# The first half's norm ahead of the shift's tiles, and the post-norm, gemv and attention steps around it re-placed

## The chip, the cores and the metric

The kernel runs on one core of a Trainium2 chip. The metric is device microseconds of one execution. A profiled execution gives the trace, whose times are microseconds from the start of its span.

## What is computed

One inference step of a trunk of two layers with D = 1024, over 640 tokens: 512 latent and 128 context. Every layer is a half-step SwiGLU FFN, a token mixer (layer 0 a Fourier mix, layer 1 attention), and another half-step FFN. Every one of these six sublayers (n = 0 to 5) sits between two RMS norms, with shift, scale and gate from a modulation vector:

```python
def _rmsnorm(x, g):
    return x * lax.rsqrt(jnp.mean(x * x, axis=-1, keepdims=True) + RMS_EPS) * g

def _modulated_prenorm(x, g, m, k):
    return _rmsnorm(x, g) * (1 + m[:, 3 * k + 1, None]) + m[:, 3 * k, None]

def _swiglu(h, w1, w2):
    gate, up = jnp.split(h @ w1, 2, axis=-1)
    return (jax.nn.silu(gate) * up) @ w2

def _half_ffn(x, m, k, g_pre, g_post, w1, w2):
    h = _modulated_prenorm(x, g_pre, m, k)
    return x + 0.5 * m[:, 3 * k + 2, None] * _rmsnorm(_swiglu(h, w1, w2), g_post)
```

Here `m = silu(cond) @ w_mod + b_mod` holds nine vectors of 1024 per layer and condition.

## The kernel before, in words

**Layout.** Activations lie transposed, channels on partitions in 8 chunks of 128, tokens along the row. The tokens are worked in two halves of 320; half 1 goes one stage behind half 0, so that one half's norms run beside the other half's matmuls. Every fp32 product is three matmuls (`mm3`, L215 to L217): a weight block and an activation block are each split into `hi` (a rounded copy, made by ACT: L195 for weights, L209 for activations) and `lo` (the rest, a subtraction on DVE: L196, L210), and hi*hi, hi*lo and lo*hi are added. A weight comes in units of 128x1024 (512 KB) by DMA on SP's queue; `unit` sends them up to three ahead of use.

**The beginning** (`begin`, L286). First the scale and the shift of sublayer 0 are needed: 16 tiles of `w_mod_k`, 512 KB each, eight of the scale (idx 1), then eight of the shift (idx 0). TensorE multiplies each as it lands (L299, 4 matmuls of 256 columns). After the scale's tiles half 0's x is loaded on SP's queue (L316, four transfers); its squares (ACT L377, L380), their sum (TensorE L419) and the spread of the inverse root (TensorE L428, after DVE L422 and POOL L423) are put between the shift's tiles, after k = 4 and 6. After tile 16 come ACT L305, TensorE L308, DVE L312 and the coefficients (L358); then per pair of chunks x times the root (DVE L453), times scale plus shift (DVE L459, ACT L461), and the split (ACT L209, DVE L210).

**The first FFN products.** `w1((0, 1), half)` takes four units at once through `multi`, which goes chunk by chunk over all four.

**The norms** (`inverse_rms`, L404) are generators: `yield` gives a time in ns of TensorE work after which the next step is put into the stream, so the sum, the spread and the scaling get places between matmuls. `pre` is the norm ahead of a sublayer, `post` the one behind it. With `in_turn` the sum and the spread keep their place behind the last matmul issued.

**The FFN's tail.** Two late blocks (f = 20, 21, `LATE`) keep a third operand, mixed weights, which `send` splits as a unit of kind "mix" when `tail` asks for it. `behind` lets background work (256 gemv instructions of the modulation, DVE L345, two to a job, one job being one `w_mod_t` tile) run along the w2 passes: 36, 28, 32 and 8 jobs for n = 0, 2, 3 and 5.

**Attention.** `products` makes q and k of the first two pairs for half 0; their evictions (DVE L910, L929, ACT likewise) are issued right behind the matmuls. Then two quads of v follow, while half 1's post norm of sublayer 3 and pre norm of sublayer 4 are finished.

Of the kernel before, what the change touches and what calls it, by code (L numbers as in the profile page):

```python
# [18 lines left out]
P = 128  # L19
# [90 lines left out]
class Kernel:  # L110
# [54 lines left out]
    def send(self, kind, src):  # L165

        nc, two, one = self.nc, slice(512, UNIT), slice(0, 512)
        at = slice(0, UNIT)  # L170
        if kind in ("plain", "block", "gate"):
            raw = self.raw_tile(src)
            self.fast["gate"] = raw
        elif kind == "sums":
            up, gate = self.raw_tile(src), self.fast["gate"]
            raw = self.raw.tile([P, UNIT], F32, tag="raw", name=self.name("sums"))
            nc.vector.tensor_tensor(raw[:, one], gate[:, one], up[:, one], op=ALU.add)
            nc.vector.tensor_tensor(up[:, one], up[:, one], up[:, two], op=ALU.add)
            nc.vector.tensor_tensor(raw[:, two], gate[:, one], up[:, one], op=ALU.add)
            self.fast["up"], self.fast["sums"] = up, raw  # L180
        elif kind in ("up", "u2"):
            raw = self.fast["up"]
            at = at if kind == "up" else two
        elif kind == "mix":
            raw = self.mixed.pop(0)
# [5 lines left out]
        if kind in ("block", "mix"):  # L191
            hi, lo = (self.ring(F32R)[:, :n] for _ in range(2))
        else:
            hi, lo = (self.wts.tile([P, UNIT], F32R, tag=tag, name=self.name(tag))[:, :n] for tag in ("hi", "lo"))
        nc.scalar.activation(hi, raw[:, at], AF.Copy)  # L195
        nc.vector.tensor_tensor(lo, raw[:, at], hi.bitcast(F32), op=ALU.subtract)  # L196
        if kind == "u2":
            nc.vector.scalar_tensor_tensor(out=raw[:, two], in0=self.fast["sums"][:, two], scalar=-1.0,
                                           in1=self.fast["gate"][:, two], op0=ALU.mult, op1=ALU.subtract)
            self.mixed.append(raw)  # L200
        return hi, lo

# [83 lines left out]
    def begin(self):  # L286


        nc, io = self.nc, self.io
        self.new_x(0)  # L290
        ps = self.bank("turn")
        sel = self.ident.rearrange("p (j r) -> p j r", j=4)[:, :, :2]
        for idx in (1, 0):
            out = ps[:, idx * 256 : (idx + 1) * 256]
            for k in range(NCH):
                raw = self.wts.tile([P, UNIT], F32, tag=("hi", "lo")[k % 2], name=self.name("first"))
                nc.sync.dma_start(out=raw, in_=io["w_mod_k"][idx, k])
# [24 lines left out]
        for c in range(0, NCH, 2):  # L322
            nc.sync.dma_start(out=self.xpair(0, c, 1), in_=io["x"][:, c : c + 2, HALF:])
        nc.sync.dma_start(out=self.wide, in_=io["cond_rows"].unsqueeze(0).to_broadcast([P, 2, D]))
        self.later = [partial(nc.scalar.activation, self.wide, self.wide, AF.Silu)]
        self.launch(1, self.pre(0, 0, 1), 4000)

# [75 lines left out]

    def inverse_rms(self, acc):  # L404

# [3 lines left out]
        if not final:  # L409
            with high():  # L410
                nc.vector.tensor_tensor(acc[:, 0], acc[:, 0], acc[:, 1], op=ALU.add)
            acc = [acc[:, 0]]
            yield 1800
        in_turn = lambda: self.tc.issue_after(self.latest.ins) if self.latest else ExitStack()
# [9 lines left out]
        yield 2200  # L424
        ps = self.bank("sum")
# [11 lines left out]

    def pre(self, layer, sub, half, acc=None):

# [25 lines left out]
    def post(self, layer, sub, half, acc, last):  # L465

        nc = self.nc
        lo, hi = SPAN[half]
        r = yield from self.inverse_rms(acc)
        final = type(r) is tuple  # L470
# [19 lines left out]
    def ffn(self, layer, which, base, boundary):  # L490
# [4 lines left out]
        begun = [False, False]  # L495
        g, sums, kept = {}, {}, {}
        quad = lambda t: t.rearrange("p (c t) -> p c t", c=4)
# [5 lines left out]
        def w1(fs, half):  # L503
# [3 lines left out]
            pss = []  # L507
            if len(fs) == 1:
                for j in range(2):
                    pss.append(self.proj(self.unit(base + self.w1_at[fs[0]] + j), lambda k: k * P, half,  # L510
                                         kind="score" if fs[0] == 2 else "main"))
            else:
                pss = self.multi([self.unit(base + self.w1_at[f] + j) for f in fs for j in range(2)], half)
# [39 lines left out]
        def product(f, ps, unit, at, x, start):  # L553
            w = self.unit(base + self.w1_at[f] + unit)
# [50 lines left out]
        def tail(f):  # L605
            a, q = kept[f]
            mix = self.mix_at[f] - self.w1_at[f]
            two(f, a, q, one(f, a, mix), mix, 512)

# [27 lines left out]
        for op, a, half in self.ffn_plan:  # L637
# [29 lines left out]
    def plan_ffn(self):  # L667
# [8 lines left out]
        for f in FAST:  # L676
            plan += [("fast", f, None)]
            if f == SLICES[due][1]:
                for m in range(NCH):
                    plan += [("w2", (due, m), 0), ("w2", (due, m), 1)]  # L680
                due += 1
        plan += [("x", None, None)]
        for half in (0, 1):
# [4 lines left out]
        self.ffn_plan = plan  # L688
        self.ffn_units, self.w1_at, self.w2_at, self.mix_at = [], {}, {}, {}
        for op, v, half in plan:  # L690
            if op == "fast":
                self.w1_at[v] = len(self.ffn_units)
                self.ffn_units += [("gate", v, 0), ("sums", v, 1)]
                self.ffn_units += [(kind, None, None) for kind in (("u2",) if v in LATE else ("up", "all"))]
            elif op == "tail":
                self.mix_at[v] = len(self.ffn_units)
                self.ffn_units += [("mix", None, None)]
            elif op == "w1":
# [181 lines left out]
    def attention(self, base, boundary):  # L880
# [91 lines left out]
        def products(jobs, half=None):  # L972

            todo = []
            for job in jobs:
# [5 lines left out]
            for k in range(NCH):  # L981
                for ps, w, t in todo:
# [8 lines left out]
            with self.tc.high_priority():  # L991
                for job, (ps, w, t) in zip(jobs, todo):
                    if t is None:
                        {"q": query, "k": key}[job[0]](job[1], half, ps)
                    else:
                        v_out(job[1], t, ps)

# [4 lines left out]
        for c in (0, 1):  # L1002
            open_pair(c)
            cached(c)
        products([("q", 0), ("k", 0), ("q", 1), ("k", 1)], 0)
# [5 lines left out]
        products([("q", 0), ("k", 0), ("v", 0, 3), ("v", 0, 4)], 1)  # L1011
        double(0)
# [265 lines left out]
```

## Time and profile before

| | |
|---|---|
| median of the runs | 2323.05 us |
| lowest, highest (3 runs) | 2320.82, 2323.87 us |
| the profiled execution | 2319.2 us |
| its span | 2317.4 us |
| mean granted clock of TensorE | 0.995 |
| TensorE busy | 98% |
| VectorE (DVE), ScalarE (ACT) busy | 75%, 55% |

The profiled execution is 1.8 us longer than its span, and 3.85 us under the median. In the rows below a line of a timeline is: start, time, engine, line, operation, output and inputs, partitions and shape, number of instructions, and in brackets how long the engine was idle before it and what ended that.

### The profile page before, as it was taken

To read this page: it belongs to the slowest core of one execution; us is meant where nothing else is said; L and a number is where in the kernel's file an instruction comes from. 1 tells how busy PE (TensorE), PEld (TensorE's weight loads), DVE (VectorE), ACT (ScalarE), POOL (GpSimd) and SP (SyncE) were. 2 spreads that over 40 slices of the span, in tenths; PEclk is the share of its full clock that TensorE was granted. 3 is DMA by queue.
4 is the path that set the end of the run, shared out by engine and by line. 5 is a ranking of instruction groups with operands and counts; after the bars stand their busy time and mean duration, and the time that the engine had idled before them with its cause. 6 is when DMAs were issued, how large, how long until landed. Compare 5 with 4: busy or idle time off the path is not lost.

```text
span 2317.4 us, 39267 instructions
## 1 busy us (share of the span) xinstructions
PE 2260.0 (98%) x15660; PEld 2209.5 (95%) x15660; DVE 1731.6 (75%) x3006; ACT 1275.8 (55%) x2456; POOL 46.5 (2%) x64
## 2 busy tenths in 40 slices
PE   6999999999999999999999999989999999999997
PEld 4999999999999999999999999988988899999997
DVE  4888888688787787768978887777667485766664
ACT  4445544565654554556545554657667664545544
POOL 0000000000000000000000000010000000000000
PEclk9999999999999999999999999999999999999998
DMA  8234443524333433353243442524333223322332
GB/s 299 94 110 154 147 129 108 182 86 122 125 107 103 139 123 119 112 174 127 86 131 121 146 120 99 189 75 147 101 101 100 83 74 101 110 92 82 101 108 75
DMA packets 80280, 278.12 MB, mean 120 GB/s; under 512 B 8800, under 2 KB 15200, under 8 KB 79968
## 3 DMA queue, kind: packets, MB, share of 16 engines
q1 hardware_dynamic: 79824, 275.29, 36.6%
q8 instruction: 122, 2.00, 0.3%
q14 instruction: 62, 0.51, 0.1%
q10 hardware_dynamic: 272, 0.33, 0.0%
HBM read 264.04 MB, written 11.53 MB: 119 GB/s over the span
## 4 chain that ended last, share of the span: by engine, by line
PE 87%; DVE 4%; ACT 4%; DMA 3%; issue 1%; POOL 0%; SPq 0%; DVEq 0%; ACTq 0%; POOLq 0%
PE main L215 25%; PE main L217 25%; PE main L216 25%; PE score L215 3%; PE score L217 3%; PE score L216 3%; DMA raw<-in_w 2%; DVE lo L196 1%; PE sum L428 1%; PE turn L1093 1%; ACT hi L195 1%; PE sum L1109 1%; DMA first<-in_w_mod_k 1%; PE sum L419 1%; PE score L1067 1%
## 5 line engine op out<-in xcount | busy, mean ns | idle before, releaser
L215 PE MATMUL main<-ring,hi 128*128 128x320 f32 x3872 | 1203.7, 312 | 9.6 <-ACT ring L209 9.6
L216 PE MATMUL main<-ring,hi 128*128 128x320 f32 x3872 | 1197.4, 310 | 0.2 <-DVE ring L210 0.2
L217 PE MATMUL main<-ring,lo 128*128 128x320 f32 x3872 | 1195.3, 309 | 1.6 <-DVE lo L196 1.6
L215 PEld LDWEIGHTS main<-ring,hi 128*128 128x128 f32 x3872 | 726.7, 188 | 16.5 <-ACT ring L209 11.8
L216 PEld LDWEIGHTS main<-ring,hi 128*128 128x128 f32 x3872 | 727.8, 188 | 1.6 <-DVE ring L210 0.9
L217 PEld LDWEIGHTS main<-ring,lo 128*128 128x128 f32 x3872 | 726.8, 188 | 1.9 <-DVE lo L196 1.9
L195 ACT ACTIVATE hi<-raw 128x1024 fp32r<-128x1024 f32 (+1 forms) x366 | 355.4, 974 | 445.0 <-PE main L216 372.0
L196 DVE TENSOR_TENSOR lo<-raw,hi 128x1024 fp32r<-128x1024 f32 (+1 forms) x366 | 408.2, 1118 | 139.6 <-ACT hi L195 138.5
L345 DVE SCALAR_TENSOR_TENSOR junk<-raw,wide 128x1024 bf16<-128x1024 f32 x256 | 312.6, 1221 | 16.3 <-DMA raw<-in_w_mod_t 13.7
L631 ACT ACTIVATE y<-main 128x320 f32<-128x320 f32 x320 | 137.3, 431 | 152.1 <-PE main L217 151.2
L196 DVE TENSOR_TENSOR lo<-sums,hi 128x1024 fp32r<-128x1024 f32 x72 | 88.0, 1222 | 60.7 <-ACT hi L195 60.7
L619 ACT ACTIVATE main<-y 128x320 f32<-128x320 f32 x256 | 111.5, 439 | 33.2 <-DVE left L600 26.2
L215 PE MATMUL score<-ring,hi 128*128 128x320 f32 x416 | 128.6, 309 | 0.0
L216 PE MATMUL score<-ring,hi 128*128 128x320 f32 x416 | 128.5, 309 | 0.0
L217 PE MATMUL score<-ring,lo 128*128 128x320 f32 x416 | 128.5, 309 | 0.0
L195 ACT ACTIVATE hi<-sums 128x1024 fp32r<-128x1024 f32 x72 | 76.3, 1060 | 28.7 <-PE main L216 17.4
L215 PE MATMUL main<-ring,ring 128*128 128x320 f32 x288 | 90.1, 313 | 0.0
L216 PE MATMUL main<-ring,ring 128*128 128x320 f32 x288 | 89.2, 310 | 0.0
L217 PE MATMUL main<-ring,ring 128*128 128x320 f32 x288 | 89.2, 310 | 0.0
L381 DVE TENSOR_TENSOR total<-total,square 128x640 f32<-128x640 f32 x71 | 58.2, 822 | 40.4 <-ACT square L380 38.7
L574 DVE TENSOR_TENSOR left<-left,main 128x320 f32<-128x320 f32 x72 | 35.0, 486 | 59.5 <-PE main L217 59.5
L216 PEld LDWEIGHTS score<-ring,hi 128*128 128x128 f32 x416 | 78.1, 188 | 0.0
(177 smaller groups left out, 2654.2 us busy)
## 6 DMA issues: line engine op xcount, KB each, us to landing
raw<-in_w SPq DMA_DIRECT2D x264, 512.0 KB, 3.6
raw<-in_w_mod_t SPq DMA_DIRECT2D x128, 512.0 KB, 4.0
raw<-in_qkv SPq DMA_DIRECT2D x26, 512.0 KB, 3.6
first<-in_w_mod_k SPq DMA_DIRECT2D x16, 512.0 KB, 8.7
spill<-ring SPq DMA_DIRECT2D x12, 640.0 KB, 3.5
ring<-spill SPq DMA_DIRECT2D x12, 640.0 KB, 7.3
raw<-in_bias SPq DMA_DIRECT2D x16, 448.0 KB, 3.4
raw<-in_four_in SPq DMA_DIRECT2D x8, 512.0 KB, 3.5
```

The costliest lines, as they stand in the source:

```text
L195: nc.scalar.activation(hi, raw[:, at], AF.Copy)
L196: nc.vector.tensor_tensor(lo, raw[:, at], hi.bitcast(F32), op=ALU.subtract)
L215: mm(out, whi, xhi, start=start, stop=False)
L216: mm(out, whi, xlo, start=False, stop=False)
L217: self.latest = mm(out, wlo, xhi, start=False, stop=stop)
L345: last = self.nc.vector.scalar_tensor_tensor(out=self.junk, in0=raw, scalar=1.0, in1=self.wide[:, cond, :], op0=ALU.mult, op1=ALU.mult, ac ...
L381: nc.vector.tensor_tensor(acc, acc, sq, op=ALU.add)
L419: nc.tensor.matmul(ps[:, j : j + 1], acc[0][:, t : t + P], self.mean, start=True, stop=True)
L428: self.spread = nc.tensor.matmul(ps[:, t : t + P], col[:, j : j + 1].to_broadcast([P, P]), self.ident, start=True, stop=True)
L574: tt(a, q, z, op=ALU.subtract)
L619: nc.scalar.activation(ps[:, :HALF], self.y[:, m, lo:hi], AF.Copy)
L631: nc.scalar.activation(self.y[:, m, lo:hi], ps[:, :HALF], AF.Copy)
```

## The change

It loads half 0's x first, on ACT's queue, and works its norm in a generator `first`, whose steps are put between the scale's tiles (after k = 3, 5 and 7). After the scale's coefficients y is multiplied by the scale; after the shift's, the shift is added in the split itself: ACT writes `hi` = t + shift, DVE writes `lo` = (t + shift) - hi. The y that the FFN needs later gets its shift from eight ACT instructions in `later`. The first unit of weights is asked for after the shift's tile k = 4, so its transfer goes ahead of the last three tiles. Half 1's norm waits 6500 ns where it waited 1800. For half 0 of sublayer 0 the four w1 units go one by one. The late blocks' mixed weights are split right behind the last slice but one. The background jobs are spread over 64 w2 passes where it was 72. `post` of half 1 waits 2800 ns ahead of the spread where it was 2200 (not behind the mixers). In attention the evictions of the first q and k are called ahead of the second quad.

```diff
 def begin(self):
         self.new_x(0)
+        for c in range(0, NCH, 2):
+            nc.scalar.dma_start(out=self.xpair(0, c, 0), in_=io["x"][:, c : c + 2, :HALF])
+        chain = self.first()
+        next(chain)
...
-                if idx == 0 and k in (4, 6):
-                    self.step(0)
+                if idx == 1 and k in (3, 5, 7):
+                    next(chain)
+                if idx == 0 and k == 4:
+                    self.unit(0, 0)
...
-            if idx:
-                for c in range(0, NCH, 2):
-                    nc.sync.dma_start(out=self.xpair(0, c, 0), in_=io["x"][:, c : c + 2, :HALF])
-                self.launch(0, self.pre(0, 0, 0), 0)
-                self.step(0)
-        with self.tc.high_priority():
-            self.finish(0)
-        self.unit(0, 3)
...
+            with self.tc.high_priority():
+                next(chain, None)
+        with self.tc.issue_after(load.ins), self.tc.issue_after(self.shifted.ins):
+            self.unit(0, 3)
...
+        self.launch(1, self.pre(0, 0, 1, fold=6500), 4000)
+
+    def first(self):
...
+        r = yield from self.inverse_rms(acc)
+        for c in range(0, NCH, 2):
+            nc.vector.tensor_tensor(self.pair(self.y, c, 0), self.xpair(0, c, 0),
+                                    r[:, :HALF].unsqueeze(1).to_broadcast([P, 2, HALF]), op=ALU.mult)
+        yield
...
+                nc.vector.tensor_scalar(t, t, scale, None, op0=ALU.mult)
+            else:
+                nc.scalar.activation(t, t, AF.Copy, scale=scale)
+        yield
+        for c in range(NCH):
+            t, shift, scale = part(c)
+            hi, lo = h.chunk(c, 0)
+            self.shifted = nc.scalar.activation(hi, t, AF.Identity, bias=shift)
+            nc.vector.scalar_tensor_tensor(out=lo, in0=t, scalar=shift, in1=hi.bitcast(F32), op0=ALU.add,
+                                           op1=ALU.subtract)
+        self.later = [partial(nc.scalar.activation, t, t, AF.Identity, bias=shift)
+                      for t, shift, scale in map(part, range(NCH))]
...
 def post(self, layer, sub, half, acc, last):
-        r = yield from self.inverse_rms(acc)
+        r = yield from self.inverse_rms(acc, 2800 if half and sub != 1 else 2200)
...
 def w1(fs, half):
-            if len(fs) == 1:
+            if len(fs) == 1 or n == half == 0:
+                for f in fs:
+                    for j in range(2):
+                        w = self.unit(base + self.w1_at[f] + j)
+                        with self.tc.issue_after(self.latest.ins):
+                            pss.append(self.proj(w, lambda k: k * P, half, kind="score" if f == 2 else "main"))
...
+            elif op == "mix":
+                mixes[a] = self.mix()
...
-                if a[0] < len(SLICES) - 1 or half == 0:
+                if a[0] < len(SLICES) - 1:
                     passed += 1
-                    due = min(BEHIND[n], BEHIND[n] * passed // (2 * NCH * (len(SLICES) - 1) + (NCH if n < 5 else 0)))
+                    due = BEHIND[n] * passed // (2 * NCH * (len(SLICES) - 1))
...
+        put = products([("q", 0), ("k", 0), ("q", 1), ("k", 1)], 0)
         for quad in (1, 0):
             while not self.normed[1][1 - quad]:
                 self.step(1)
+            if quad == 0:
+                put()
             v_tiles(quad, (0, 1), early, "score")
```

How the instructions lie on three engines, before and after. First ACT at the beginning, from the copy of the inverse root (L432, now L467) to the second weight split (L195, now L194); L305 (now L316) copies a product with `w_mod_k`. Before:

```order
L432 ACTIVATE rms_31_235<-sum_30_231 128x320
L305 ACTIVATE left_33_243<-turn_6_106 128x256
L195 ACTIVATE hi_40_278<-raw_39_276 128x1024
L461 ACTIVATE y_78<-y_78,coef_83 128x320 x2
L209 ACTIVATE ring_35_255<-y_78 128x640 x2
L461 ACTIVATE y_78<-y_78,coef_83 128x320 x2
L209 ACTIVATE ring_37_267<-y_78 128x640 x2
L195 ACTIVATE hi_43_284<-raw_42_282 128x1024
```

After:

```order
L467 ACTIVATE rms_20_170<-sum_19_166 128x320
L316 ACTIVATE left_23_188<-turn_10_122 128x256
L352 ACTIVATE y_78<-y_78,coef_83 128x320 x4
L194 ACTIVATE hi_31_239<-raw_30_237 128x1024
L316 ACTIVATE left_36_261<-turn_10_122 128x256
L357 ACTIVATE ring_38_270<-y_78,coef_83 128x320 x4
L357 ACTIVATE ring_40_280<-y_78,coef_83 128x320 x4
L194 ACTIVATE hi_43_292<-raw_42_290 128x1024
```

The root, the scale's multiplications and the first weight split now stand ahead of the shift's L316; behind it only the eight L357 remain.

Second DVE in attention, from the last eviction of the first q and k (L929, now L965) to the fold of half 1's squares for sublayer 4's norm (L411, now L446). L381 (now L416) adds squares, L477 and L479 (now L512 and L514) are the post norm's x times root and its addition. Before:

```order
L929 TENSOR_TENSOR ring_2226_15839<-main_2239_15865,ring_2226_15839 64x192
L381 TENSOR_TENSOR total_2247_15939<-total_2247_15939,square_2248_15961 128x640
L477 TENSOR_TENSOR y_78<-y_78,rms_2246_15926 128x2x320
L196 TENSOR_TENSOR lo_2242_15869<-raw_2240_15866,hi_2241_15868 128x1024
L479 TENSOR_TENSOR ring_2145_15241<-ring_2145_15241,y_78 128x2x320
L196 TENSOR_TENSOR lo_2255_16031<-raw_2253_16028,hi_2254_16030 128x1024
L381 TENSOR_TENSOR total_2247_15939<-total_2247_15939,square_2249_15981 128x640
L381 TENSOR_TENSOR total_2247_15939<-total_2247_15939,square_2250_16022 128x640
L954 COPY square_2251_16026<-score_2259_16040 128x128
L411 TENSOR_TENSOR total_2247_15939<-total_2247_15939 128x320
```

After:

```order
L965 TENSOR_TENSOR ring_2226_15855<-main_2239_15881,ring_2226_15855 64x192
L416 TENSOR_TENSOR total_2247_15958<-total_2247_15958,square_2248_15980 128x640
L416 TENSOR_TENSOR total_2247_15958<-total_2247_15958,square_2249_16003 128x640
L195 TENSOR_TENSOR lo_2242_15885<-raw_2240_15882,hi_2241_15884 128x1024
L416 TENSOR_TENSOR total_2247_15958<-total_2247_15958,square_2250_16014 128x640
L195 TENSOR_TENSOR lo_2255_16023<-raw_2253_16020,hi_2254_16022 128x1024
L446 TENSOR_TENSOR total_2247_15958<-total_2247_15958 128x320
```

The evictions still stand ahead of the squares' additions. The last pair's L477 and L479, which stood between the two, now stand ahead of the evictions, and a copy (L954) is behind the fold.

Third TensorE behind those squares: their sum (L419, now L454) and spread (L428, now L463); the rest are v's matmuls. Before:

```order
L217 MATMUL score_2260_16067<-hi_2237_15861,ring_2220_15827 128x256
L419 MATMUL sum_2261_16094<-mean_86,total_2247_15939 128x1 x3
L215 MATMUL score_2273_16128<-hi_2241_15868,ring_2210_15762 128x256
L216 MATMUL score_2273_16128<-lo_2242_15869,ring_2210_15762 128x256
L428 MATMUL sum_2263_16101<-ident_85,col_2262_16098 128x128 x3
```

After:

```order
L222 MATMUL score_2260_16059<-hi_2237_15877,ring_2220_15843 128x256
L454 MATMUL sum_2261_16086<-mean_86,total_2247_15958 128x1 x3
L463 MATMUL sum_2263_16093<-ident_85,col_2262_16090 128x128 x3
L220 MATMUL score_2273_16144<-hi_2241_15884,ring_2210_15778 128x256
L221 MATMUL score_2273_16144<-lo_2242_15885,ring_2210_15778 128x256
```

The two matmuls between the sum and the spread are gone.

## Rows read from the trace of the kernel before

**Rows 1.** Part 1 of the page: busy time, share of the span, instructions of an engine.

```profile
PE 2260.0 (98%) x15660; PEld 2209.5 (95%) x15660; DVE 1731.6 (75%) x3006; ACT 1275.8 (55%) x2456; POOL 46.5 (2%) x64
```

**Rows 2.** Timeline of TensorE (PE) at the beginning.

```profile
25.07 1.08 PE L299 MATMUL turn<-first,right 128*32 128x256 f32 x8 [0.21 <-DMA first<-in_w_mod_k]
...
29.32 1.65 PE L428 MATMUL sum<-ident,col 128*128 128x128 f32 x6
30.89 1.08 PE L299 MATMUL turn<-first,right 128*32 128x256 f32 x8
...
36.43 0.64 PE L215 MATMUL main<-ring,hi 128*128 128x320 f32 x1 [2.92 <-ACT ring L209]
...
39.54 0.64 PE L217 MATMUL main<-ring,lo 128*128 128x320 f32 x1 [1.60 <-DVE lo L196]
39.97 0.47 PE L215 MATMUL main<-ring,hi 128*128 128x320 f32 x1
40.24 0.47 PE L216 MATMUL main<-ring,hi 128*128 128x320 f32 x1
...
42.64 0.39 PE L217 MATMUL main<-ring,lo 128*128 128x320 f32 x1
...
51.88 0.93 PE L428 MATMUL sum<-ident,col 128*128 128x128 f32 x6 [1.59 <-POOL col L423]
```

**Rows 3.** Timeline of TensorE: spreads of two post norms, then one pre norm's end.

```profile
489.50 0.93 PE L428 MATMUL sum<-ident,col 128*128 128x128 f32 x6 [0.63 <-POOL col L423]
...
1078.42 0.94 PE L428 MATMUL sum<-ident,col 128*128 128x128 f32 x6 [0.71 <-POOL col L423]
...
1099.12 0.80 PE L419 MATMUL sum<-mean,total 128*128 128x1 f32 x6
...
1105.60 0.85 PE L215 MATMUL main<-ring,hi 128*128 128x320 f32 x4 [0.85 <-ACT ring L209]
```

**Rows 4.** Timeline of TensorE in attention.

```profile
1538.08 0.28 PE L217 MATMUL score<-hi,ring 128*128 128x256 f32 x1
...
1544.72 1.41 PE L419 MATMUL sum<-mean,total 128*128 128x1 f32 x6 [6.37 <-DVE total L411]
...
1547.45 1.65 PE L428 MATMUL sum<-ident,col 128*128 128x128 f32 x6 [0.68 <-POOL col L423]
...
1549.97 0.41 PE L216 MATMUL score<-lo,ring 128*128 128x256 f32 x1
```

**Rows 5.** SP's queue at the beginning: its DMA issues.

```profile
1.65 4.32 SPq L297 DMA_DIRECT2D first<-in_w_mod_k  x8
```

**Rows 6.** Windows: stretch, length, busy PE, PEld, DVE, ACT, POOL, clock, DMA share, GB/s.

```profile
20.00:25.00 5.00, 4.27 (x32) 0.75 (x32) 1.45 (x3) 0.00 (x0) 0.00 (x0) 1.00 1.02 409
170.00:180.00 10.00, 10.00 (x70) 10.00 (x70) 6.51 (x10) 5.25 (x8) 0.00 (x0) 1.00 0.57 166
```

**Rows 7.** Timeline of DVE: first modulation copy behind tile 16; fold of sublayer 2's pre norm.

```profile
33.54 0.17 DVE L312 COPY mod<-score 128x8 f32<-128x8 f32 x1 [0.51 <-PE score L308]
...
34.36 0.16 DVE L358 TENSOR_TENSOR coef<-mod,vec 128x8 f32<-128x8 f32 x1
...
1098.49 0.48 DVE L411 TENSOR_TENSOR total<-total 128x320 f32<-128x320 f32 x1
```

**Rows 8.** Groups of ACT by form: busy us, mean ns; one pointer operand (L401).

```profile
L401 ACT ACTIVATE y<-y,coef 128x320 f32<-128x320 f32 x48 | 24.9, 555 | 0.6
```

**Rows 9.** Timeline of DVE in attention.

```profile
1522.10 1.23 DVE L196 TENSOR_TENSOR lo<-raw,hi 128x1024 fp32r<-128x1024 f32 x1 [0.22 <-ACT hi L195]
1524.31 0.82 DVE L477 TENSOR_TENSOR y<-y,rms 128x640 f32<-128x640 f32 x1 [0.98 <-ACT rms L432]
...
1532.92 0.99 DVE L910 SCALAR_TENSOR_TENSOR ring<-main,ring 64x320 fp32r<-64x320 f32 x2
...
1537.62 0.83 DVE L381 TENSOR_TENSOR total<-total,square 128x640 f32<-128x640 f32 x1
```

**Rows 10.** Part 5 of the page, background jobs: busy us, mean ns, idle before.

```profile
L345 DVE SCALAR_TENSOR_TENSOR junk<-raw,wide 128x1024 bf16<-128x1024 f32 x256 | 312.6, 1221 | 16.3 <-DMA raw<-in_w_mod_t 13.7
```

More of the change, by code (lines that the diff above doesn't have):

```diff
@@ L190, in send @@
         n = at.stop - at.start
-        if kind in ("block", "mix"):
+        if kind == "block":
             hi, lo = (self.ring(F32R)[:, :n] for _ in range(2))
@@ L200, in send, with mix @@
             self.mixed.append(raw)
+        return hi, lo
+    def mix(self):
+        raw = self.mixed.pop(0)
+        hi, lo = (self.ring(F32R)[:, :UNIT] for _ in range(2))
+        self.split(hi, lo, raw)
         return hi, lo
@@ L296, in begin @@
                 raw = self.wts.tile([P, UNIT], F32, tag=("hi", "lo")[k % 2], name=self.name("first"))
-                nc.sync.dma_start(out=raw, in_=io["w_mod_k"][idx, k])
+                load = nc.sync.dma_start(out=raw, in_=io["w_mod_k"][idx, k])
                 for j in range(4):
@@ L324, in begin @@
-        nc.sync.dma_start(out=self.wide, in_=io["cond_rows"].unsqueeze(0).to_broadcast([P, 2, D]))
-        self.later = [partial(nc.scalar.activation, self.wide, self.wide, AF.Silu)]
-        self.launch(1, self.pre(0, 0, 1), 4000)
+            with self.tc.high_priority():
[3 more added lines that the diff above has]
+            for c in range(0, NCH, 2):
+                nc.sync.dma_start(out=self.xpair(0, c, 1), in_=io["x"][:, c : c + 2, HALF:])
+            nc.sync.dma_start(out=self.wide, in_=io["cond_rows"].unsqueeze(0).to_broadcast([P, 2, D]))
@@ new lines, in begin @@
+        self.later.insert(0, partial(nc.scalar.activation, self.wide, self.wide, AF.Silu))
+        self.launch(1, self.pre(0, 0, 1, fold=6500), 4000)
+    def first(self):
+        nc, h = self.nc, self.hs[0]
+        acc = None
+        for c in range(0, NCH, 2):
+            acc = self.sum_square(acc, self.xpair(0, c, 0))
+        r = yield from self.inverse_rms(acc)
+        for c in range(0, NCH, 2):
+            nc.vector.tensor_tensor(self.pair(self.y, c, 0), self.xpair(0, c, 0),
+                                    r[:, :HALF].unsqueeze(1).to_broadcast([P, 2, HALF]), op=ALU.mult)
+        yield
+        part = lambda c: (self.y[:, c, :HALF], self.coef[:, 0, 0, 0, 0, c : c + 1], self.coef[:, 0, 0, 1, 0, c : c + 1])
+        for c in range(NCH):
+            t, shift, scale = part(c)
+            if c % 2:
+                nc.vector.tensor_scalar(t, t, scale, None, op0=ALU.mult)
+            else:
+                nc.scalar.activation(t, t, AF.Copy, scale=scale)
+        yield
+        for c in range(NCH):
+            t, shift, scale = part(c)
+            hi, lo = h.chunk(c, 0)
[4 more added lines that the diff above has]
+                      for t, shift, scale in map(part, range(NCH))]
@@ L402, in weigh, with inverse_rms @@
         return acc
-    def inverse_rms(self, acc):
+    def inverse_rms(self, acc, root=2200, fold=1800):
         nc = self.nc
@@ L412, in inverse_rms @@
             acc = [acc[:, 0]]
-            yield 1800
+            yield fold
         in_turn = lambda: self.tc.issue_after(self.latest.ins) if self.latest else ExitStack()
@@ L423, in inverse_rms @@
             nc.gpsimd.tensor_tensor(col, col, self.power, op=ALU.pow)
-        yield 2200
+        yield root
         ps = self.bank("sum")
@@ L436, in inverse_rms, with pre @@
         return r
-    def pre(self, layer, sub, half, acc=None):
+    def pre(self, layer, sub, half, acc=None, fold=1800):
         nc = self.nc
@@ L445, in pre @@
                 acc = self.sum_square(acc, self.xpair(n, c, half))
-        r = yield from self.inverse_rms(acc)
+        r = yield from self.inverse_rms(acc, fold=fold)
         self.normed[half][1] = True
@@ L495, in ffn @@
         begun = [False, False]
-        g, sums, kept = {}, {}, {}
+        g, sums, kept, mixes = {}, {}, {}, {}
         quad = lambda t: t.rearrange("p (c t) -> p c t", c=4)
@@ L553, in product @@
         def product(f, ps, unit, at, x, start):
-            w = self.unit(base + self.w1_at[f] + unit)
+            w = mixes[f] if unit is None else self.unit(base + self.w1_at[f] + unit)
             for k in range(4):
@@ L606, in tail @@
             a, q = kept[f]
-            mix = self.mix_at[f] - self.w1_at[f]
-            two(f, a, q, one(f, a, mix), mix, 512)
+            two(f, a, q, one(f, a, None), None, 512)
         acc = [None, None]
@@ L681, in plan_ffn @@
                 due += 1
+        plan += [("mix", f, None) for f in LATE]
         plan += [("x", None, None)]
@@ L990, in products, with put @@
                         self.mm3(ps[:, :256], *a, w[k // 4][0][:, ws], w[k // 4][1][:, ws], k == 0, k == NCH - 1)
[L991 to L996, printed above, removed]
+            def put():
+                with self.tc.high_priority():
+                    for job, (ps, w, t) in zip(jobs, todo):
+                        if t is None:
+                            {"q": query, "k": key}[job[0]](job[1], half, ps)
+                        else:
+                            v_out(job[1], t, ps)
+            return put
         steps = self.attend(pairs, ctx_qk, values)
@@ L1008, in attention @@
                 self.step(1)
+            if quad == 0:
+                put()
             v_tiles(quad, (0, 1), early, "score")
         self.finish(1)
-        products([("q", 0), ("k", 0), ("v", 0, 3), ("v", 0, 4)], 1)
+        products([("q", 0), ("k", 0), ("v", 0, 3), ("v", 0, 4)], 1)()
         double(0)
```

13 lines of the change are left out of this document (1 added, 12 removed).

## The prediction

> **What bounds the kernel now.** The shares come first: TensorE is busy 2260.0 us, 98% of the span, DVE 75% [rows 1]. So a gain must come out of TensorE's idle time, some 57 us (2317.4 - 2260.0), or make it run faster; no matmul of the products is removed. Then the timeline of TensorE shows where that idle time lies and who ends it. Most of it is at the beginning, where no products run yet [rows 2]; single waits of half a microsecond to one stand behind the norms [rows 3], and one of 6.37 us in attention [rows 4]. Last come the queues and DVE, to see whether what TensorE would wait for next can be had sooner.
>
> At the beginning the reader should see two different limits. In the stretch 20 to 25 the DMA engines are fully used, 409 GB/s at a share of 1.02 [rows 6], so a 512 KB tile comes every 524288 / 409000 = 1.28 us, and TensorE waits for each [rows 2]. Tile 13 is taken at 25.07, so tile 16 could be taken at 25.07 + 3 x 1.28 = 28.91; but half 0's spread stands in front of it (29.32, 1.65 us), and tile 16 starts at 30.89. From there it is a chain of waits: tile 16 ends at 31.97, the first product starts at 36.43, the third, which needs the weight's `lo`, at 39.54. DVE and ACT have a whole norm to do in that gap.
>
> **The change, part by part.** All is reckoned against the profiled execution (2319.2 us) and then moved to the median, which stands 3.85 us higher.
>
> *Tile 16.* The norm goes ahead, so the spread is off this place. x's bytes come before the tiles rather than between them: no difference in bytes. The first w1 unit is put ahead of the last three tiles: one unit, +1.28 us. Against it, SP issued the first tile at 1.65 [rows 5], behind two small transfers; x now starts on ACT's queue beside them. That is worth up to about 0.9 us, at worst nothing. Tile 16 is then taken between 28.91 + 1.28 - 0.9 = 29.3 and 30.2. I take 29.8, ending at 29.8 + 1.08 = 30.9, where it ended at 31.97: **1.1 us** (0.7 to 1.6).
>
> That rests on 409 GB/s at a share of 1.02 [rows 6]: a second queue adds no bandwidth here. The Trainium skill, "DMA: Bandwidth & Descriptors", section "Issuing engines are not separate DMA queues", says that transfers started by different engines run on the same 16 DMA engines, and that starting them from two saves only the sequencer's time to issue, usually small. By that rule the 0.9 us would be nothing and the sum 0.4 us less; no run here shows yet which holds.
>
> *From tile 16 to the products.* Before: 36.43 - 31.97 = 4.46 us. Of it 1.57 us, from 31.97 to DVE's first small copy at 33.54 [rows 7], remain: ACT's L316 and TensorE's L319. Then two small DVE operations of 0.17 us or less remain, overlapped, about 0.4 us to the first coefficient; x times root and times scale are done earlier, in time in which DVE is busy 1.45 and ACT 0.00 of 5 us [rows 6]. What follows is one ACT instruction of 128x320 with a pointer operand, 0.555 us by the like one [rows 8]. Sum 1.57 + 0.4 + 0.56 = 2.5, I take 2.6 for semaphores. First product at 30.9 + 2.6 = 33.5: **1.9 us** more (1.2 to 2.2).
>
> *The third matmul.* The slow pace at the beginning is 40.24 - 39.97 = 0.27 us a matmul. The third would have been due at 36.43 + 2 x 0.27 = 36.97 and came at 39.54: **2.6 us**. With the first unit split ahead of the shift, nothing is left to wait for. The slow pace holds until about 42.64, 3.1 us after the matmuls became steady, and is 0.27 rather than the 0.143 of a stretch with 70 in 10 us [rows 6]. I leave its cost as it is; were it to last 6.2 us from the first product, some 11 matmuls more would be slow, 11 x 0.127 = 1.4 us lost.
>
> *Half 1's spread.* It waits 1.59 us for POOL at 51.88 [rows 2]. The later place (6500 ns for 1800) gives its squares and root time: **1.6 us** (at worst 0, if the squares come later as well). Against it: the units go one by one, so unit 2 needs its split after 24 matmuls, where four units shared 96. I take 0.3 us for such a wait; a weight split costs 1.23 on DVE [rows 9], which bounds it. The eight L559 on ACT (8 x 0.56 = 4.4 us) run beside products and nobody waits for them soon.
>
> Beginning: 1.1 + 1.9 + 2.6 + 1.6 - 0.3 = **6.9 us**, between 4.5 and 8.5.
>
> *Post norms.* The spread of half 1 after sublayer 0 waits 0.63 for POOL, after sublayer 2 0.71 [rows 3]; with 600 ns more both waits go: 0.63 + 0.71. After sublayer 2 the next norm's sum then stands 19 matmuls earlier in TensorE's order, 19 x 0.143 = 2.7 us, while the fold it needs ends at 1098.49 + 0.48 [rows 7]. The sum stood at 1099.12 [rows 3]; 2.7 and 0.71 us earlier is 95.7 in that clock, so it could wait up to 3.3 us. Three DVE instructions move behind the fold, so I take 1.1. In return the wait of 0.85 at 1105.60 for ACT's split goes, as the root is there sooner. 0.63 + 0.71 + 0.85 - 1.1 = **1.1 us** (-1.1 to 2.2). After sublayer 3 the wait is swallowed by attention's, below.
>
> *Attention.* TensorE is idle 6.37 us until DVE's fold of half 1's squares [rows 4]. The evictions stand before those additions: 1537.62 - 1532.92 = 4.7 us of DVE [rows 9]. The words of the change would take them out of the way, but the order of the changed kernel has them in the same place; only the last pair's scaling went past them, and DVE's work up to the fold is the same but for one weight split (1.23) moved into an earlier idle time, the idle 0.98 and 0.22 us at 1524.31 and 1522.10 filled, and a copy less. 1.23 + 0.98 + 0.2 = 2.4 us sooner; of the 0.22 I count nothing. Against it the spread follows its sum with no matmul between. Before, the sum ended at 1544.72 + 1.41 = 1546.13 and POOL's wait began at 1547.45 - 0.68 = 1546.77 [rows 4]; the two matmuls between filled at most 0.64 us, and since they overlap I take 0.4 us of longer wait. **2.0 us** (0 to 2.4).
>
> *Mixed weights and gemv jobs.* The split of two units moves ahead by a few; nothing is added, and DVE and ACT have idle time there. The jobs are as many as before, more densely placed: 36 over 64 passes, not 72. In 170 to 180 DVE is busy 6.51 of 10 us [rows 6] with such jobs. Nothing, unless the cover fails (below).
>
> **Sum**: 6.9 + 1.1 + 2.0 = 10.0 us, 2309.2 for a profiled execution, 2313.0 for the median.
>
> **Rivals.** *More* (chance 0.17): the attention wait closes. If the scheduler's order lets ACT and DVE get past the evictions, up to 4.0 us of remaining wait goes too, and the slow pace behind it: 0.41 against 0.28 for a matmul [rows 4], the sum and spread likewise (1.41 and 1.65 against 0.80 and 0.94, [rows 3, 4]), some 2.5 us. 2313.0 - 4.0 - 2.5 = 2306.5. Against it: the order as printed.
>
> *Part given back* (0.22): x on a second queue gives nothing and delays the scale's tiles, the slow pace lasts, unit 2 waits a whole split, the earlier sum waits its full 3.3 us. 4.5 - 1.1 + 2.0 = 5.4, so 2317.7; with attention's gain gone too, 2319.7.
>
> *The change doesn't do what it says* is part of the forecast for the evictions; for the beginning the order shows that it does.
>
> *Slower* (0.05): the denser gemv jobs make DVE the bound. Of 72 passes 8 lay behind the last slice but one, so a ninth of the jobs of sublayers 0, 2 and 3 (36 / 9 = 4, 28 / 9 = 3.1, 32 / 9 = 3.6) now goes into earlier passes, at 2 x 1.221 = 2.44 us each [rows 10]: together 10.7 x 2.44 = 26 us if DVE had no idle time left. 2313 + 26 = 2339. It decides from the point where a slice's DVE idle time falls under one job, 2.44 us. Against it: 10.00 - 6.51 = 3.5 us idle in 10 us with jobs in them [rows 6].
>
> Some 0.06 is left for no effect at all, mishaps that cancel the gain.
>
> **How the numbers follow.** The forecast, 0.50, lies between 2309 and 2317. The range 2305.5 to 2319.5 takes in *more* and nearly all of *part given back*. A measurement can tell about 0.2%, 4.6 us, from no change, so faster means under 2318.4: the forecast, *more*, and three fourths of *part given back*, 0.84. Same: the rest of it and the mishaps, 0.11. Slower: 0.05.
>
> **What would show it.** First product at 33 to 34; the third directly behind it; no wait at half 1's first spread; the waits at the post spreads gone and one of about a microsecond at sublayer 2's next sum; attention's wait at about 4 us with the slow pace still behind it; the same idle time as before elsewhere. A first product after 35, a new wait in the first 30 us of products, or DVE releasing TensorE in the w2 passes would make the prediction wrong.

## The result and the profile after

The changed kernel took 2307.91 us (median of 4; 2307.49 to 2309.2) beside 2321.94 before, a ratio of 0.9944 (95% interval 0.9930 to 0.9958). A later comparison (the changed kernel again, below) gave 0.995 (0.9937 to 0.9962). By these ratios it is 12 to 13 us faster; the medians differ by 14.0 and 10.9. The two profiled executions differ by 2319.2 - 2309.2 = 10.0 us.

TensorE in the changed kernel, timeline, beginning (answers to [rows 2]):

```profile
28.90 2.79 PE L308 MATMUL turn<-first,right 128*32 128x256 f32 x24 [3.75 <-DMA first<-in_w_mod_k]
...
33.92 0.41 PE L220 MATMUL main<-ring,hi 128*128 128x320 f32 x1 [1.11 <-ACT ring L357]
...
34.76 0.30 PE L222 MATMUL main<-ring,lo 128*128 128x320 f32 x1
```

The last three tiles are taken together, behind 3.75 us without work; they end at 31.69, only 0.3 us sooner than tile 16 did. The semaphores in the trace show what TensorE waited for. The three transfers landed at 26.25, 28.86 and 30.14, and TensorE's first wait is for the second of them: in its order the second tile stands ahead of the first, which lay ready for 2.65 us. The first product follows 2.2 us later (before 4.46), the third has no wait of its own, and half 1's spread (at 49.44) shows none. The windows (columns as in [rows 6]) tell why three tiles took 2.79 us:

```profile
20.00:25.00 5.00, 4.50 (x60) 2.11 (x52) 4.62 (x14) 1.81 (x5) 0.00 (x0) 1.00 1.03 411
...
29.00:32.00 3.00, 2.69 (x24) 0.89 (x24) 0.00 (x0) 0.24 (x1) 0.00 (x0) 0.52 1.02 405
```

The granted clock stands at 0.52 there, close to 1.2 of 2.4 GHz, after the idle time; the DMA engines are full as before.

Later in the same timeline (answers to [rows 3, 4]):

```profile
426.56 0.56 PE L220 MATMUL main<-ring,hi 128*128 128x320 f32 x2 [1.84 <-ACT ring L214]
...
428.25 0.47 PE L220 MATMUL main<-ring,hi 128*128 128x320 f32 x1
428.52 0.47 PE L221 MATMUL main<-ring,hi 128*128 128x320 f32 x1
...
1090.04 0.93 PE L463 MATMUL sum<-ident,col 128*128 128x128 f32 x6 [0.94 <-POOL col L458]
...
1534.45 1.41 PE L454 MATMUL sum<-mean,total 128*128 128x1 f32 x6 [4.76 <-DVE total L446]
1537.18 1.65 PE L463 MATMUL sum<-ident,col 128*128 128x128 f32 x6 [1.32 <-POOL col L458]
```

The product of the first row started at 433.10 before:

```profile
433.10 0.56 PE L215 MATMUL main<-ring,hi 128*128 128x320 f32 x2 [1.75 <-ACT ring L209]
```

So 6.5 us are gained by here. The waits of 0.63, 0.71 and 0.85 [rows 3] are gone; attention's wait is 4.76 for 6.37, the one behind it 1.32 for 0.68.

Both traces hold 15660 matmuls, so the nth of one can be set beside the nth of the other. The changed kernel is ahead by 6.6 us once half 1's first norm is done, by 7.3 behind sublayer 0, by 9.6 behind sublayer 2, by only 7.1 in the last FFN slice before attention, by 10.3 in attention and by 10.0 at the end. The 2.5 us lost before attention stand behind this wait, which was 1.41 before; the granted clock falls behind it (0.96 in 1440 to 1480, where it read 1.00 before):

```profile
1457.37 0.56 PE L220 MATMUL main<-ring,hi 128*128 128x320 f32 x2 [2.04 <-ACT ring L214]
```

DVE in the last FFN slice before attention and on to its sum, windows of the kernel before and of the changed one:

```profile
1466.00:1545.00 79.00, 71.28 (x494) 70.01 (x494) 64.49 (x98) 55.26 (x112) 7.64 (x7) 0.98 0.47 157
```

```profile
1457.00:1536.00 79.00, 73.73 (x498) 72.60 (x498) 55.30 (x82) 55.30 (x112) 5.91 (x7) 0.96 0.39 128
```

DVE does 64.49 us of work before and 55.30 after: the eight gemv instructions (9.8 us) that lay in this stretch now run in earlier slices.

### The profile page after: what moved, and what is told of

Same layout as the page of the kernel before. It is cut to its first block, busy times and chain, and to the rows that moved or that the text cites. A ratio compares the mean times of both kernels' runs of the same rounds, so it can differ in the third digit from the quotient of the medians.

```text
span 2307.4 us, 39285 instructions
## 1 busy us (share of the span) xinstructions
PE 2254.9 (98%) x15660; PEld 2211.1 (96%) x15660; DVE 1733.1 (75%) x3010; ACT 1279.0 (55%) x2468; POOL 42.6 (2%) x64
## 3 DMA queue, kind: packets, MB, share of 16 engines
q10 hardware_dynamic: 1360, 1.64, 0.2%
## 4 chain that ended last, share of the span: by engine, by line
PE 88%; ACT 4%; DVE 4%; DMA 3%; issue 1%; POOL 0%; DVEq 0%; SPq 0%; ACTq 0%; POOLq 0%
PE main L220 25%; PE main L221 25%; PE main L222 25%; PE score L220 3%; PE score L222 3%; PE score L221 3%; DMA raw<-in_w 2%; DVE lo L195 1%; ACT hi L194 1%; PE turn L1135 1%; PE sum L463 1%; PE sum L1151 1%; PE sum L454 1%; PE score L1109 1%; ACT left L1095 1%
## 5 line engine op out<-in xcount | busy, mean ns | idle before, releaser
L194 ACT ACTIVATE hi<-raw 128x1024 fp32r<-128x1024 f32 (+1 forms) x366 | 356.3, 976 | 442.7 <-PE main L221 357.3
L195 DVE TENSOR_TENSOR lo<-raw,hi 128x1024 fp32r<-128x1024 f32 (+1 forms) x366 | 408.5, 1117 | 146.5 <-ACT hi L194 145.0
L416 DVE TENSOR_TENSOR total<-total,square 128x640 f32<-128x640 f32 x71 | 58.4, 824 | 85.1 <-ACT square L415 83.8
L195 DVE TENSOR_TENSOR lo<-sums,hi 128x1024 fp32r<-128x1024 f32 x72 | 88.0, 1222 | 42.7 <-ACT hi L194 42.6
L194 ACT ACTIVATE hi<-sums 128x1024 fp32r<-128x1024 f32 x72 | 76.4, 1061 | 31.5 <-DVE sums L180 14.0
L214 ACT ACTIVATE ring<-right 128x320 fp32r<-128x320 f32 x104 | 48.0, 470 | 56.2 <-DVE right L620 35.3
```

The costliest lines, as they stand in the source:

```text
L214: self.nc.scalar.activation(hi, src, AF.Copy)
L416: nc.vector.tensor_tensor(acc, acc, sq, op=ALU.add)
```

## The experiments

Four kernels at a time shared a chip with runs of the kernel before; ratios are to that kernel. Edits are shown against the changed kernel, and in part where `...` stands.

**The beginning alone** (the late edits undone).

```diff
-        r = yield from self.inverse_rms(acc, 2800 if half and sub != 1 else 2200)
+        r = yield from self.inverse_rms(acc, 2200)
...
-                if a[0] < len(SLICES) - 1:
+                if a[0] < len(SLICES) - 1 or half == 0:
...
-        plan += [("mix", f, None) for f in LATE]
...
-            if quad == 0:
-                put()
```

> The changed kernel with its late parts undone: mixed weights, gemv pacing, the post norms' 2200 ns and the evictions as before, so that the beginning alone is changed. Theory: the parts add up, and the beginning gives what the traces show up to the second sublayer's w2 pass (433.10 against 426.56): 6.5 us less than the kernel before, and TensorE's wait in attention stays at 6.4 us. Rival: the beginning carries nearly all of it (10 to 13 us less), because the denser jobs and moved norms give nothing.

2312.31 against 2317.91, ratio 0.9977 (0.9968 to 0.9986): 5.3 us less. The interval takes in the theory's 6.5 and leaves out the rival's 10. Attention's wait is the old one:

```profile
1539.83 1.41 PE L456 MATMUL sum<-mean,total 128*128 128x1 f32 x6 [6.36 <-DVE total L448]
```

**The late edits alone** (`begin` and `w1` as before).

```diff
-            if len(fs) == 1 or n == half == 0:
+            if len(fs) == 1:
...
-        chain = self.first()
+                self.launch(0, self.pre(0, 0, 0), 0)
```

> The changed kernel with the beginning undone (x loaded behind the scale's tiles, the norm among the shift's tiles, four units at once, half 1 at 1800 ns). Theory: what the traces show behind the first FFN, 3.5 us less than the kernel before, of it 2.4 up to the attention (post norms and what goes with them) and about 1 in attention. Rival: 6 to 7 us less, if the medians' 13 to 14 us are true and the beginning is 6.5 of them.

2312.65, ratio 0.9977 (0.9966 to 0.9987): 5.3 us less, between the two expectations; the interval, 3 to 8 us, takes in both. The parts add up to 10.6, and each is about half.

**The first unit behind the last tile.**

```diff
-                if idx == 0 and k == 4:
+                if idx == 0 and k == 7:
```

> The changed kernel, but the first w1 unit's transfer is asked for behind the shift's last tile and not ahead of the last three. Theory: tile 16's landing is set by the bytes ahead of it, so the last three tiles come 1.28 us sooner, TensorE's idle stretch of 3.75 us before them shortens by as much, and the first product starts 1.0 to 1.5 us sooner, at 32.4 to 32.9, unless its split is late; total 1 us less than the changed kernel. Rival: the unit then lands last, its two splits (1.04 and 1.23 us) stand between it and the third product, and the first products start at 33.9 or later: 0 to 1.5 us more.

Ratio 0.9958 (0.9946 to 0.9971), no better than the changed kernel. The tiles came sooner and were taken in the order of their landing, each behind its own short wait, but the unit is now what is late:

```profile
27.70 0.64 PE L308 MATMUL turn<-first,right 128*32 128x256 f32 x8 [1.20 <-DMA first<-in_w_mod_k]
28.99 0.64 PE L308 MATMUL turn<-first,right 128*32 128x256 f32 x8 [0.65 <-DMA first<-in_w_mod_k]
...
36.38 0.64 PE L220 MATMUL main<-ring,hi 128*128 128x320 f32 x1 [5.22 <-ACT hi L194]
```

The rival held in the trace: the first product starts 2.5 us later than in the changed kernel (33.92), so the one tile's delay that the change accepts for this unit is well paid there. The two ratios do not separate. This is the only run with the new beginning in which the three tiles are in order, so the price of their order in the other runs was not tried by itself.

**The evictions really deferred.**

```diff
             def put():
-                with self.tc.high_priority():
+                with ExitStack() if half == 0 else self.tc.high_priority():
```

> The changed kernel, but the deferred evictions of the first q and k are issued without priority, so that on DVE and ACT the squares, their additions and the fold pass most of them. Theory: the evictions are what holds the fold; it ends about 5 us sooner (1534.3 becomes about 1529), TensorE's wait of 4.76 us goes, and the slow pace behind it (sum 1.41, spread 1.65, some ten matmuls) too: 5 to 7 us less than the changed kernel. Rival: the evictions come later than the next products need their banks, and a new wait of 2 to 4 us stands there: 1 to 3 us less.

2301.39, ratio 0.9931 (0.9918 to 0.9943): 16 us less than before and, by the ratios, 3 to 4 less than the changed kernel. The wait for the fold is gone, two smaller ones stand there:

```profile
1526.21 0.39 PE L221 MATMUL score<-lo,ring 128*128 128x256 f32 x1 [1.38 <-DVE lo L195]
1528.11 1.59 PE L463 MATMUL sum<-ident,col 128*128 128x128 f32 x6 [1.40 <-POOL col L458]
```

The intervals of this ratio and the changed kernel's overlap, but a later run with the same deferral (the splits behind the last fast block's, below) lies in all five executions (2303.59 to 2305.69) under all five of the changed kernel beside it (2305.84 to 2312.65). So the evictions were what held the fold, and the change as written did not move them.

**The changed kernel again**, without an edit.

> The changed kernel itself, beside the kernel before on the same chip, with more executions. [...] Rival: the parts help each other and 13 to 14 us stay.

2309.62 against 2320.56, ratio 0.995 (0.9937 to 0.9962): 10.9 us less by the medians. That is about the sum of the two parts run alone (5.3 and 5.3); the 14.0 between the first medians did not come again.

**DVE's splits behind the last fast block's** (on top of the real deferral). `hold` is the split of the last fast block; one of its weight units is also asked for later.

```diff
...
+        with self.tc.issue_after(self.hold.ins) if self.hold else ExitStack():
             nc.scalar.activation(hi, raw[:, at], AF.Copy)
             nc.vector.tensor_tensor(lo, raw[:, at], hi.bitcast(F32), op=ALU.subtract)
```

> The kernel of the low-priority evictions, and in the FFNs' last fast block the two weight splits that stood ahead of the last product's multiplication on DVE now stand behind its split. Theory: the four waits of 0.8 to 2 us in the last slices (at about 425, 1011, 1453 and 2235) come from that order, DVE waiting for a weight's transfer ahead of work that TensorE wants; they go, and with them the falls of the granted clock: 4 to 8 us less than the kernel of the low-priority evictions, some 10 to 13 less than the changed one. Rival: the splits are then late for the last slice's own products, and the waits reappear there: 0 to 2 us less.

2304.02, ratio 0.993 (0.9916 to 0.9943), as without it, so the rival held. The wait in the last slice stayed (2.10 us). ACT's timeline shows who took DVE's place, a weight's copy (L195) that waits for its transfer ahead of the split (L216):

```profile
423.74 1.06 ACT L195 ACTIVATE hi<-raw 128x1024 fp32r<-128x1024 f32 x1 [1.90 <-DMA raw<-in_w]
...
425.06 0.45 ACT L216 ACTIVATE ring<-right 128x320 fp32r<-128x320 f32 x1
```

**Post norms at 2200 ns.**

```diff
-        r = yield from self.inverse_rms(acc, 2800 if half and sub != 1 else 2200)
+        r = yield from self.inverse_rms(acc, 2200)
```

> The changed kernel with 2200 ns again ahead of the post norms' spread. Theory: the waits of 0.63 and 0.71 us for POOL come back, the one at the next sum (here none was seen, so the expected 1.1 us is not given back) stays away: 1.3 to 2.2 us more than the changed kernel. Rival: no difference, as the 0.85 us for ACT's split and the wait for POOL at the pre norm trade against each other.

2310.48, ratio 0.9953 (0.9941 to 0.9966), within the error of the changed kernel, and none of the waits for POOL at the post norms came back: the spread that waited 0.63 before starts at 484.53 with its input ready. The 2800 ns did not remove them.

**x first, on SP's queue.**

```diff
-            nc.scalar.dma_start(out=self.xpair(0, c, 0), in_=io["x"][:, c : c + 2, :HALF])
+            nc.sync.dma_start(out=self.xpair(0, c, 0), in_=io["x"][:, c : c + 2, :HALF])
```

> The changed kernel with x loaded first, but on SP's queue ahead of the scale's tiles. Theory: the queue doesn't matter, since the DMA engines are full from the first microseconds and tile 16 is due when the bytes ahead of it are through: SP issues the four transfers in about 2 us and the first tile is that much later, but the landing of tile 16 moves by no more than 0.5 us; 0 to 0.5 us more. Rival: the second queue is worth its issue time, 1 to 2 us more than the changed kernel.

2309.36, ratio 0.9952 (0.994 to 0.9964): no difference that is measured. In the trace SP issues the four transfers in 1.96 us from 1.64 on. Tile 16 lands at 31.77, 1.6 us later than in the changed kernel's two traces (30.14 and 30.19), so the theory's 0.5 at most fails there, and the last tiles are taken 1.6 us later than in the trace beside it (28.95):

```profile
30.53 2.79 PE L308 MATMUL turn<-first,right 128*32 128x256 f32 x24 [2.76 <-DMA first<-in_w_mod_k]
```

The Trainium skill ("DMA: Bandwidth & Descriptors", section "Issuing engines are not separate DMA queues") says that initiating DMAs on several engines saves only the sequencer's time to initiate them. The trace agrees: 1.96 us of issue, and tile 16 later by 1.6. In the medians it is lost.

**The gemv pacing undone.**

```diff
-                if a[0] < len(SLICES) - 1:
+                if a[0] < len(SLICES) - 1 or half == 0:
...
-                    due = BEHIND[n] * passed // (2 * NCH * (len(SLICES) - 1))
+                    due = min(BEHIND[n], BEHIND[n] * passed // (2 * NCH * (len(SLICES) - 1) + (NCH if n < 5 else 0)))
```

> The changed kernel with the gemv jobs spread over 72 passes again, the last slice's first half among them; post norms at 2800 ns, mixed weights and evictions stay changed. Theory: what freed DVE behind the FFNs and in attention is that the last slice's passes carry no jobs, not the 2800 ns and not the evictions' place; without it TensorE waits 6.4 us in attention again, and nearly all of the late parts' gain goes, 4 to 6 us more than the changed kernel. Rival: the pacing is worth nothing, as I reckoned, and the kernel stays within 1 us of the changed one.

2324.39 against 2320.75, ratio 1.0016 (1.0007 to 1.0025): slower than the kernel before, and 0.0066 or 15 us slower than the changed kernel, three times what was expected. TensorE's timeline:

```profile
474.90 0.93 PE L463 MATMUL sum<-ident,col 128*128 128x128 f32 x6 [1.15 <-POOL col L458]
487.33 0.94 PE L463 MATMUL sum<-ident,col 128*128 128x128 f32 x6 [0.64 <-POOL col L458]
...
1079.75 1.30 PE L463 MATMUL sum<-ident,col 128*128 128x128 f32 x6 [1.22 <-POOL col L458]
...
1551.96 1.41 PE L454 MATMUL sum<-mean,total 128*128 128x1 f32 x6 [6.50 <-DVE total L446]
```

With the 2800 ns and the edit on the evictions in place, every wait is back (0.70 and 0.86 at sublayer 2's pre norm too), and there are new ones. The window behind the third of these rows shows what a wait costs on top, a granted clock of 0.91 over 20 us with TensorE busy throughout:

```profile
1080.00:1100.00 20.00, 20.00 (x129) 20.00 (x129) 16.25 (x24) 9.49 (x15) 0.00 (x0) 0.91 0.67 234
```

**The splits held on ACT too** (on top of the real deferral; for two weight splits, with units asked for later).

```diff
...
+        with self.tc.issue_after(self.hold[0].ins) if self.hold else ExitStack():
             nc.scalar.activation(hi, raw[:, at], AF.Copy)
+        with self.tc.issue_after(self.hold[1].ins) if self.hold else ExitStack():
             nc.vector.tensor_tensor(lo, raw[:, at], hi.bitcast(F32), op=ALU.subtract)
```

> The kernel of the low-priority evictions, with two weight splits of the last slice behind the last fast block's split on ACT as well as on DVE (the run before moved only DVE's, and ACT's copy of a weight then held the split in DVE's place). Theory: the four waits of 1 to 2 us in the last slices go; 4 to 6 us less than the kernel of the low-priority evictions, so 20 us or more less than the kernel before. Rival: the held splits stand behind the mixed weights' and come late for the last slice's second unit, a wait of 1 to 2 us a few microseconds later: no more than 2 us less.

2317.34, ratio 0.9985 (0.9976 to 0.9993): 13 us worse than the deferral alone. The four waits did shrink, to 0.6 us, but the norms' waits came back, as with the pacing undone:

```profile
427.45 0.41 PE L225 MATMUL main<-ring,lo 128*128 128x320 f32 x1 [0.60 <-DVE lo L197]
473.19 1.34 PE L466 MATMUL sum<-ident,col 128*128 128x128 f32 x6 [1.15 <-POOL col L461]
...
1077.88 0.94 PE L466 MATMUL sum<-ident,col 128*128 128x128 f32 x6 [1.21 <-POOL col L461]
```

Neither expectation held; 2 to 3 us saved were paid many times over behind. And no gemv job lies in the last slices here, so the jobs are not the only thing that brings these waits. What the runs that have them share is TensorE's order: a spread stands close behind its sum. In the changed kernel 14 matmuls of the products lie between the two, and the spread does not wait:

```profile
468.23 0.80 PE L454 MATMUL sum<-mean,total 128*128 128x1 f32 x6
...
471.02 0.83 PE L463 MATMUL sum<-ident,col 128*128 128x128 f32 x6
```

Before, 6 lay between this pair, with a wait of 0.20; with the pacing undone and in this run 3, with a wait of 1.15 each. The sum itself stands 15 matmuls later in the order before than in the changed kernel, 24 and 23 later in these two runs. That a later DVE moves it there is argued, not shown.

**Four units at once.**

```diff
-            if len(fs) == 1 or n == half == 0:
+            if len(fs) == 1:
```

> The changed kernel, but half 0's first four units go through the chunks together again. Theory: taking them one by one is what lets the first products start without the other units' splits, which end at 39 to 42; together, the fourth product of a chunk waits for them, 3 to 5 us more. Rival: the order is free to take what is there, as before, and only the waits of a split or two show: within 1.5 us of the changed kernel.

2310.69, ratio 0.9954 (0.994 to 0.9967): the rival held, no difference is measured.

**Half 1's first sum after 1800 ns.**

```diff
-        self.launch(1, self.pre(0, 0, 1, fold=6500), 4000)
+        self.launch(1, self.pre(0, 0, 1), 4000)
```

> The changed kernel with half 1's first sum after 1800 ns again. Theory: its sum then stands ahead of DVE's fold (which ends at about 45.8) and TensorE waits for it or for POOL, 1.6 us or more as before the change: 1.5 to 4 us more. Rival: the sum keeps its place behind the products and nothing changes.

2313.27, ratio 0.9966 (0.9953 to 0.9978), 0.0016 or 3.7 us above the changed kernel's 0.995. The intervals overlap; the trace is the firmer sign, with the old wait to the hundredth:

```profile
48.86 1.33 PE L463 MATMUL sum<-ident,col 128*128 128x128 f32 x6 [1.59 <-POOL col L458]
```

## Why the prediction was right, and where it was not

The forecast was 10.0 us; 10.0 between the profiled executions, 10.9 and 14.0 between medians. The time lies in the range. It lies under 2309, though, in the band that the prediction gave to *more*, whose mechanism did not come: attention's wait is still 4.76. That the profiled pair agrees to a tenth is luck. The profiled execution before was faster than all four of the comparison (2319.68 at least), the one after the slowest of its four, and the terms missed on both sides.

- **Tile 16**, 1.1 us: 0.3. Two things took the rest. The tile landed at 30.14 where 29.8 was taken, within the bounds; the reckoning let the tiles land 1.28 apart, while before, too, the last one landed at 29.38 and not at 28.91. And the step took the tiles to be used one by one as they land. In TensorE's order two of them were swapped, so both were worked from 28.90 on, at half clock behind 3.75 us of idle time, and tile 16 was done 1.55 us after it landed, where the prediction had 1.08. **The second queue**, 0.9 at most: 1.6 in the trace of the run without it.
- **From tile 16 to the products**, 1.9: 4.46 - 2.23 = 2.2. **Third matmul**, 2.6: no wait, right. **Half 1's spread**, 1.6: right, and 3.7 by the run with 1800 ns, where the clock in 40 to 60 is 0.91. **The price of one unit after the other**, 0.3: nothing seen. The beginning was to give 6.9; the traces say 6.5, the run of it alone 5.3.
- **Post norms**, 1.1, and **attention**, 2.0: the late edits alone gave 5.3, with the 3.1 at the edge of the interval. In the traces the stretches give 3.0 and 3.2, and the slice between gives back 2.5, which no term had. The waits that were to go went, a wait of about a microsecond does stand at sublayer 2's next norm (0.94, for POOL and not for the fold), and attention's wait fell by 1.6. The sum for attention counts 0.2 us of which it says that it counts nothing; without it the term is 1.8. The step that credited the post norms' waits to the 2800 ns was wrong, as the run at 2200 shows.
- **Mixed weights and gemv jobs**, "nothing": this step failed. It asked only whether the denser passes have room on DVE, and did not ask what the emptied slice gives. That slice is where the norms' squares, folds and scalings share DVE with the jobs, and its eight gemv instructions are 9.8 us of DVE work in 79 [rows 10]. The rival that went to the slower side had its sign from the same omission: undoing the pacing, not making it, costs 15 us beside the other late edits.
- **The evictions' deferral** did not do what it says, as forecast; *more*, the rival that closes the wait in attention, needed the edit of the fourth run, and with it came to 16 us, near the 16.5 less (2306.5) of that rival.

Some things stay open. With the old pacing the kernel is 9 us slower than the beginning alone (1.0016 against 0.9977); which of the early split of the mixed weights, the 2800 ns and the edit on the evictions does that beside the jobs was not tried one by one, nor was the new pacing alone. So the 15 us are the pacing's worth in this company, not by itself. The scatter of executions, up to 7 us, fits waits of 0.7 to 2.1 us in the last slices that differ from trace to trace; that this is its whole cause is argued, not shown.

## What to carry to other kernels

Background work is priced where it leaves as well as where it goes: taken out of the stretch in which an engine carries a chain that the bottleneck waits for, it can give more than its cover elsewhere costs, as here beside the other late edits. Whether a deferral happened is read from the order of the queues, not from the place of the call in the source. The same holds for transfers: a tile that lands early gains nothing when its user stands behind the user of a later one. A local wait closed by holding instructions back can move a whole schedule: price what stands behind the held ones.

## What the hardware showed that was not expected

Short waits of TensorE cost more than themselves when the granted clock falls behind them. After the 1.84 us at 426.56 matmuls come every 0.27 us (428.25, 428.52) where 0.15 is usual, for 13 of them, some 1.6 us; the clock reads 0.91 in 420 to 440:

```profile
420.00:440.00 20.00, 18.16 (x113) 17.81 (x112) 9.38 (x10) 14.28 (x25) 0.00 (x0) 0.91 0.70 251
```

Before the change the wait of 1.75 at the same product was followed by no fall:

```profile
420.00:440.00 20.00, 18.25 (x124) 17.91 (x123) 11.36 (x17) 13.11 (x23) 0.00 (x0) 1.00 0.66 235
```

In the run with the late edits alone the wait was 1.10 and the clock 1.00. The length of the wait does not sort the cases: with the pacing undone the clock fell behind 1.22 us (at 1079.75), in the changed kernel it read 1.00 in 1010 to 1030 with a wait of 1.59 at 1014.61. The Trainium skill, "TensorE: Matmul & The Clock Gate", section "What's actually happening", says that a monitor sets the clock by how busy the engine has been recently. These traces agree in kind: the clock falls behind waits and is back while the matmuls run on (0.15 us apart again from 431.36). They add that a wait of under 2 us can be enough, and sometimes is not.
